# A hybrid decoder layer: the split parts of the key, weight and time-step matrix are kept for all four token tiles

## The chip, the cores and the metric

The kernel runs on one core of one Trainium2 chip. The core has five engines that each work through their own queue in order: TensorE (PE in the rows, its weight loads are PEld), VectorE (DVE), ScalarE (ACT), GpSimd (POOL) and SyncE (SP), which issues the DMA requests of this kernel. The metric is device time of one execution in microseconds (us). Lower is better.

## The reference, cut to what matters

One layer, 2048 tokens of width 1024. One input projection feeds an attention over selected keys and a state-space mixer (SSD); their outputs go through an output projection and an MLP.

```python
u = rms_norm(h, norm_pre_mix)
q, k, v, qi, ki, wi, z, xbc, dt = split(u @ w_in)     # widths 512,128,128,256,64,4,512,1024,8
ki = layer_norm(ki); wi = wi * 4 ** -0.5
attn = sparse_attention(q, k, v, qi, ki, wi, rel_bias)  # each query keeps its 256 best keys by
                                                        # sum_h wi[t,h] relu(qi[t,h] . ki[s])
ssd = ssd_mixer(z, xbc, dt, ...)                        # causal conv, scan over chunks of 128, gate, norm
h = h + rms_norm(concat(attn, ssd) @ w_out)
h = h + rms_norm(square(relu(rms_norm(h) @ w_up)) @ w_down)
```

The change concerns three of the nine outputs of the input projection: the index keys `ki` (64 columns), the index weights `wi` (4) and the time steps `dt` (8). Their 76 columns of `w_in` are one array, `w_misc`, of 1024 x 76.

## The kernel before

All large products are made of fp32 numbers split into a high part and a low rest (fp32r): `split` (lines 228 to 232) writes the high part with ACT (L229) or POOL (L231), by a switch, and the rest with POOL (L232). `mm3` (L257, L260, L261) then multiplies high by high, high weight by low operand, and low weight by high operand into one PSUM bank.

**The stages.** The tokens lie in four tiles of 512. The first stage, some 760 us long, runs `in_proj(t)` for the four tiles one after another. The later stages run the output projection and the MLP tile by tile. `in_proj(t)` makes 21 products with the tile's operand `u`, which has eight slices u[0] to u[7] of 128 rows each; a product `proj` is eight `mm3`, so 24 matmuls. The first product of a tile is the one with `w_misc` (76 rows out, tile `p_mm`, `mi`); then come eight products for `xbc`, two for `qi`, four for `z`, one each for `k` and `v`, and four for `q`. The slices of the next tile are made at the end of a tile by `moving(t + 1)`: for each slice a request `xr<-x_t`, a scaled copy on ACT (L305, L308, L311) and the rest on DVE (L312) or POOL (L309, slices 3, 5 and 7). There are eight buffers `u`, so slice k of the next tile can be written once the last product of the old tile has read slice k. I call the stretch from the last product of one tile to the first product with `w_in` of the next a seam; there are three.

**Weights.** `load_w` (L236 to L248) fetches a matrix in two halves of four slices each: a request `wr<-...` (L246) into one of four raw buffers `wr`, which the eight requests `xr` use too, then `split` into buffers `wh` and `wl`, two of each. `w_misc` goes this way in every tile: in tile 0 with the high part on ACT, in tiles 1 to 3 with both parts on POOL, in all four through the same `wr`, `wh` and `wl` as the other weights.

**Order.** SSD steps (`p_x`, `p_y`, `p_st`, `lm`, `cb`, `si`), the search for the best keys (`p_ix`, `junk_k`, `cnd`) and attention (`p_s`, `p_pt`, `p_o`, `qs`, `tq`) are woven into the products by `weave` with planned times. A scheduler then fixes the order of every engine's queue at build time from priorities and modelled durations; a change at one place so alters the order elsewhere. SP's requests also go out in their fixed order: one that waits for a buffer holds those behind it.

Of the kernel before, what the change touches and what calls it, by code (L numbers as in the profile page):

```python
# [21 lines left out]
P = 128  # L22
# [5 lines left out]
KT = D // P  # L28
# [13 lines left out]
def hybrid_layer(ctx, tc, x, x_t, w_cols, n_post_mix, n_post_mlp, w_in, w_misc, dt_bias, a_log, d_skip,  # L42
# [10 lines left out]
    HI_, HO, HU, HW = "00,11,00,00".split(",")  # L53
    FC, BC = (2,3)
# [4 lines left out]
    WR = 4  # L59
    COMMON = dict(u=8, wr=WR, wl=WL, wh=WL, rsb=1, sc=2, mkk=1, qi=1, ks=2)  # L60
    ATT = dict(c2=2, qs=2)
    FRONT = dict(c4=FC, x24=1, m4=2, m2=3, kc=2, tq=1, mk=1)
    BACK = dict(c4=BC, x8=2, g4=9, m2=2)
    SSD = dict(si=3, cb=2, lm=1, xd=1)
    SIDE = [dict(kc=3, tq=1, mk=1), dict(kc=2, tq=1)]
# [16 lines left out]
    def tl(tag, shape, dt=F32, name=None):  # L82
        pool, bufs, slot = place(tag)
        return pool.tile(shape, dt, tag=name if tag in ("s", "ks", "ssm") else slot, name=name or tag, bufs=bufs)

    def phase(name, sizes, smalls=None, side="left"):
        stack = ExitStack()
        pool = stack.enter_context(tc.tile_pool(name=name, bufs=1, side=side, reuse_waits="tile"))
        use(pool, sizes)
        if smalls:  # L90
            use(pool, {smalls: 2})
        return stack
# [13 lines left out]
    def banks(name, sizes):  # L106
        stack = ExitStack()
        use(stack.enter_context(tc.tile_pool(name=name, bufs=1, space=PSUM, reuse_waits="tile")), sizes)
        return stack
# [11 lines left out]
    scan = phase("scan", SSD, "ssm", "right")  # L121
    front = phase("front", FRONT, "s")
    side_banks = banks("bank0", BANKS[0])
# [103 lines left out]
    def split(dst_hi, dst_lo, src_f, how):  # L227
        if how:
            S.activation(dst_hi, src_f, AF.Copy)  # L229
        else:  # L230
            G.tensor_scalar(dst_hi, src_f, 1.0, 0.0, op0=OP.mult, op1=OP.add)  # L231
        G.tensor_tensor(dst_lo, src_f, dst_hi.bitcast(F32), op=OP.subtract)  # L232

    def load_w(ap, shape, how='00', tag=None):

        n = shape[1] // 2  # L236
        parts = []
        for i in range(2):
            raw = tl("wr", [P, n, shape[2]], name="wr")
            if tag:  # L240
                both = tl(tag, [P, 2, n, shape[2]], F32R, name="w2")
                hi, lo = both[:, 0], both[:, 1]
            else:
                hi = tl("wh", [P, n, shape[2]], F32R, name="wh")
                lo = tl("wl", [P, n, shape[2]], F32R, name="wl")
            SP.dma_start(raw, ap[:, i * n:(i + 1) * n])  # L246
            split(hi, lo, raw, how[i] == '1')
            parts.append((hi, lo))  # L248
        return parts

    state = {"win": "0"}
# [13 lines left out]
    def proj(ap, u, w=None, how='00'):  # L265

        m = ap.shape[-1]
        w = w or load_w(ap, [P, KT, m], how)
        p = pt("mm", "p_mm")
        for k in range(KT):  # L270
            hi, lo = w[k // 4]
            mm3(p[0:m], hi[:, k % 4, :], lo[:, k % 4, :], u[k][:, 0, :], u[k][:, 1, :], k == 0, k == KT - 1)
        return p
# [45 lines left out]

    def in_proj(t):  # L320
        t0 = t * T
        w = None
        if t == 0:
            w = load_w(w_misc, [P, KT, 76], '11')
            moving(0)
        else:
            rsb = row_spread(state["rs", t], TB)
        u = state["u", t]
        scaled = lambda o, p: V.tensor_tensor(o, p, rsb[0:o.shape[0]], op=OP.mult)


        p = proj(w_misc, u, w, how=HI_)
        if t == 0:
            row_scale(0)
            rsb = row_spread(state["rs", 0], "acc")
# [5 lines left out]
        p = pt(TB, "p_tr")  # L341
# [22 lines left out]
        for m in range(8):  # L364
            p = proj(w_in[m], u, how=HI_)
# [9 lines left out]
            if m == 1:  # L375
                p = pt(TB, "p_tr")
# [21 lines left out]
        for m in range(4):  # L398
            p = proj(w_in[8 + m], u, how=HI_)
# [9 lines left out]
        p = proj(w_in[12], u, how=HI_)  # L409
# [8 lines left out]
        p = proj(w_in[13], u, how=HI_)  # L418
# [3 lines left out]
        p = pt(TB, "p_tr")  # L422
# [665 lines left out]
```

## Time and profile before

| what | value |
|---|---|
| median of 3 runs | 2921.4 us (2916.97 to 2927.34) |
| the profiled execution's own time | 2928.29 us |
| its span, first to last instruction | 2926.5 us |
| mean granted TensorE clock | 0.973 of full speed |
| PE busy | 2761.9 us, 94% of the span |
| POOL, DVE, ACT busy | 1762.6, 1642.4, 1481.5 us |
| share of the chain that ended last | PE 67%, DVE 13%, ACT 6%, DMA 5%, issue 4%, POOL 3% |

The profile is of one execution. A row of the timeline gives start, duration, engine, line, operation, output and inputs, shape and count, and in brackets how long the engine had been idle and what ended that. A row of the windows gives the busy time of each engine in one stretch of the span.

### The profile page before, as it was taken

To read this page: it belongs to the slowest core of one execution; us is meant where nothing else is said; L and a number is where in the kernel's file an instruction comes from. 1 tells how busy PE (TensorE), PEld (TensorE's weight loads), DVE (VectorE), ACT (ScalarE), POOL (GpSimd) and SP (SyncE) were. 2 spreads that over 40 slices of the span, in tenths; PEclk is the share of its full clock that TensorE was granted. 3 is DMA by queue.
4 is the path that set the end of the run, shared out by engine and by line. 5 is a ranking of instruction groups with operands and counts; after the bars stand their busy time and mean duration, and the time that the engine had idled before them with its cause. 6 is when DMAs were issued, how large, how long until landed. Compare 5 with 4: busy or idle time off the path is not lost.

```text
span 2926.5 us, 41201 instructions
## 1 busy us (share of the span) xinstructions
PE 2761.9 (94%) x13558; PEld 2250.7 (77%) x13558; DVE 1642.4 (56%) x4106; ACT 1481.5 (51%) x2550; POOL 1762.6 (60%) x1721
## 2 busy tenths in 40 slices
PE   7988989789989999998999999999999999999998
PEld 5766767667768887887787888878888888778886
DVE  5479588888575666747765565666444342511113
ACT  2375477675837575677773847644332332311101
POOL 4666556667666656654456575644564656588775
PEclk8999989999989999999999999999999999999999
DMA  3765654634733333255223222553222225522222
GB/s 128 224 189 151 218 157 149 208 118 160 249 120 119 112 103 102 90 176 180 101 94 98 90 97 79 170 177 102 87 95 81 93 78 177 204 95 97 95 94 86
DMA packets 286741, 383.46 MB, mean 131 GB/s; under 512 B 26520, under 2 KB 151360, under 8 KB 286528
## 3 DMA queue, kind: packets, MB, share of 16 engines
q1 hardware_dynamic: 286528, 380.84, 40.0%
q8 instruction: 107, 1.75, 0.2%
q14 instruction: 106, 0.87, 0.1%
HBM read 316.44 MB, written 64.30 MB: 130 GB/s over the span
## 4 chain that ended last, share of the span: by engine, by line
PE 67%; DVE 13%; ACT 6%; DMA 5%; issue 4%; POOL 3%; SPq 1%; POOLq 0%; DVEq 0%; ACTq 0%
PE p_mm L257 9%; PE p_mm L261 9%; PE p_mm L260 9%; PE p_dn L260 7%; PE p_dn L261 7%; PE p_dn L257 7%; ACT junk_k L610 5%; PE p_o L725 4%; PE p_s L683 4%; PE p_pt L717 3%; POOL wl L232 2%; PE p_ix L591 1%; DVE cnd L618 1%; PE p_acc L260 1%; PE p_acc L257 1%
## 5 line engine op out<-in xcount | busy, mean ns | idle before, releaser
L232 POOL TENSOR_TENSOR wl<-wr,wh 128x512 fp32r<-128x512 f32 (+1 forms) x740 | 987.0, 1335 | 179.6 <-ACT wh L229 107.0
L231 POOL TENSOR_SCALAR wh<-wr 128x512 fp32r<-128x512 f32 x674 | 449.6, 667 | 752.1 <-PE p_mm L260 372.8
L257 PE MATMUL p_mm<-u,wh 128*128 128x512 f32 (+1 forms) x1696 | 685.4, 404 | 47.4 <-ACT u L311 15.4
L261 PE MATMUL p_mm<-u,wl 128*128 128x512 f32 (+1 forms) x1696 | 682.8, 404 | 13.2 <-POOL wl L232 12.9
L260 PE MATMUL p_mm<-u,wh 128*128 128x512 f32 (+1 forms) x1696 | 674.9, 398 | 0.6 <-POOL u L309 0.3
L610 ACT ACTIVATE junk_k<-sc,cnd 128x512 int8<-128x512 f32 (+10 forms) x434 | 576.4, 1328 | 157.8 <-DVE cnd L618 122.2
L257 PEld LDWEIGHTS p_mm<-u,wh 128*128 128x128 f32 (+1 forms) x1696 | 322.9, 190 | 119.3 <-ACT u L311 17.5
L260 PE MATMUL p_dn<-wl,g 128*128 128x512 f32 x1008 | 402.2, 399 | 4.2 <-POOL wl L232 4.2
L261 PE MATMUL p_dn<-wh,g 128*128 128x512 f32 x1008 | 399.5, 397 | 2.7 <-POOL g L836 2.7
L261 PEld LDWEIGHTS p_mm<-u,wl 128*128 128x128 f32 (+1 forms) x1696 | 322.5, 190 | 88.7 <-POOL wl L232 21.3
L260 PEld LDWEIGHTS p_mm<-u,wh 128*128 128x128 f32 (+1 forms) x1696 | 322.6, 190 | 69.6 <-DVE u L312 2.3
L257 PE MATMUL p_dn<-wh,g 128*128 128x512 f32 x1008 | 328.0, 398 | 1.9 <-POOL wh L231 1.3
L834 ACT ACTIVATE r<-r 128x512 f32<-128x512 f32 x128 | 80.4, 629 | 437.1 <-DVE r L833 436.7
L688 DVE CUSTOM_DVE_ANT_0 pp<-p_s,mk 128x512 f32<-128x512 f32 (+3 forms) x320 | 192.5, 607 | 134.3 <-PE p_s L683 130.5
L719 ACT ACTIVATE ppt<-p_pt 128x512 fp32r<-128x512 f32 (+1 forms) x288 | 155.3, 568 | 208.1 <-PE p_pt L717 170.0
L720 DVE TENSOR_TENSOR ppt<-p_pt,ppt 128x512 fp32r<-128x512 f32 (+1 forms) x288 | 182.6, 655 | 129.6 <-ACT ppt L719 126.9
L260 PEld LDWEIGHTS p_dn<-wl,g 128*128 128x128 f32 x1008 | 190.3, 189 | 46.8 <-POOL wl L232 5.5
L261 PEld LDWEIGHTS p_dn<-wh,g 128*128 128x128 f32 x1008 | 190.3, 189 | 43.8 <-POOL g L836 3.1
L257 PEld LDWEIGHTS p_dn<-wh,g 128*128 128x128 f32 x1008 | 185.8, 189 | 42.0 <-POOL wh L231 2.9
L725 PE MATMUL p_o<-ppt,VV 128*128 128x256 f32 x1088 | 211.1, 294 | 1.9 <-DVE ppt L720 1.0
L617 DVE TENSOR_SCALAR keep<-cnt 128x1 int32<-128x1 f32 (+1 forms) x341 | 70.2, 206 | 244.1 <-ACT junk_k L610 242.7
L836 POOL TENSOR_TENSOR g<-r,g 128x512 fp32r<-128x512 f32 x128 | 170.1, 1331 | 53.2 <-ACT g L835 51.9
(253 smaller groups left out, 4177.6 us busy)
## 6 DMA issues: line engine op xcount, KB each, us to landing
wr<-w_up SPq DMA_DIRECT2D x256, 256.0 KB, 2.6
wr<-w_down SPq DMA_DIRECT2D x256, 256.0 KB, 2.6
wr<-w_in SPq DMA_DIRECT2D x160, 256.0 KB, 2.9
tq<-toep_d SPq DMA_DIRECT2D x128, 128.0 KB, 2.6
qs<-q_d SPq DMA_DIRECT2D x256, 64.0 KB, 2.5
wr<-w_out SPq DMA_DIRECT2D x64, 256.0 KB, 3.7
mix<-mix_d SPq DMA_DIRECT2D x32, 512.0 KB, 8.1
q_d<-qp SPq DMA_DIRECT2D x24, 512.0 KB, 3.6
```

Of the source, the lines that this page charges most:

```text
L231: G.tensor_scalar(dst_hi, src_f, 1.0, 0.0, op0=OP.mult, op1=OP.add)
L232: G.tensor_tensor(dst_lo, src_f, dst_hi.bitcast(F32), op=OP.subtract)
L257: m = PE.matmul(o, ah, bh, start=first, stop=False)
L260: PE.matmul(o, ah, bl, start=False, stop=False)
L261: state["mm3"] = PE.matmul(o, al, bh, start=False, stop=last).ins.name
L610: S.activation(junk_k[:, 0:n], scs[j], AF.Sign, bias=bias(j), accum_out=cnt[:, j:j + 1])
L683: PE.matmul(p[:, 0:w], qs[:, var, hh, :], K1[:, g, j0:j0 + w], start=var == 0, stop=var == 1)
L688: V.tensor_tensor_reduce(out=pp[:, j0:j0 + w], in0=p[:, 0:w], in1=mk[:, j0:j0 + w], scale=1.0, scalar=-3e38, op0=OP.add, op1=OP.max, accum ...
L719: S.activation(pg[:, 0, 0:w], p[:, 0:w], AF.Copy)
L720: V.tensor_tensor(pg[:, 1, 0:w], p[:, 0:w], pg[:, 0, 0:w].bitcast(F32), op=OP.subtract)
L725: PE.matmul(po[:, c0:c0 + 256], VV[:, kk, g, :], pg[:, part, j * 256:(j + 1) * 256], start=kk == 0 and part == 0, stop=kk == nb - 1 and pa ...
L836: G.tensor_tensor(gt[:, 1, :], r, gt[:, 0, :].bitcast(F32), op=OP.subtract)
```

## The change

In tile 0 the two halves of `w_misc` are split into buffers of their own (tag `wm`, two buffers of 2 x 4 x 76 fp32, 4.9 KB per partition in all) and all four tiles read them from there. Tiles 1 to 3 make no request for `w_misc` and no split of it. In tile 0 the split itself is the same; only its place is another.

```diff
-    FRONT = dict(c4=FC, x24=1, m4=2, m2=3, kc=2, tq=1, mk=1)
+    FRONT = dict(c4=FC, x24=1, m4=2, m2=3, kc=2, tq=1, mk=1, wm=2)
...
     def in_proj(t):
         t0 = t * T
-        w = None
         if t == 0:
-            w = load_w(w_misc, [P, KT, 76], '11')
+            state["wm"] = load_w(w_misc, [P, KT, 76], '11', "wm")
             moving(0)
...
-        p = proj(w_misc, u, w, how=HI_)
+        p = proj(w_misc, u, state["wm"])
```

One line of source is gone, so lines behind L322 have a number lower by one in the changed kernel. The order of the queues moves at the seams, and in smaller steps elsewhere.

SP's requests at the seam into tile 2, before (`xr` is the last slice of `u`, `qs` and `tq` belong to attention):

```order
L676 DMA tq<-toep_d 128x256
L486 DMA cb<-cs_d_3716 128x512
L570 DMA qs<-q_d 64x2x128 x4
L676 DMA tq<-toep_d 128x256
L393 DMA q_d<-qp 128x2x512
L301 DMA xr<-x_t 128x512
L246 DMA wr<-w_misc 128x304
L676 DMA tq<-toep_d 128x256
L246 DMA wr<-w_misc 128x304
L755 DMA mix_d<-atp 128x4x128
L246 DMA wr<-w_in 128x512
```

and now:

```order
L675 DMA tq<-toep_d 128x256
L485 DMA cb<-cs_d_3702 128x512
L301 DMA xr<-x_t 128x512
L246 DMA wr<-w_in 128x512
L569 DMA qs<-q_d 64x2x128 x4
L675 DMA tq<-toep_d 128x256
L392 DMA q_d<-qp 128x2x512
L246 DMA wr<-w_in 128x512
L675 DMA tq<-toep_d 128x256
L246 DMA wr<-w_in 128x512 x2
```

The last slice and the first half of the first matrix of `w_in` have moved ahead of the four `qs`, one `tq` and the `q_d` request.

POOL at the same seam, before (`u` here is slice 5, then slice 7; the splits of `w_misc` have 304 columns):

```order
L501 TENSOR_TENSOR xd<-xd,ends 128x256
L504 TENSOR_TENSOR cb<-cb,si 128x512
L309 TENSOR_TENSOR u<-xr,u 128x512
L231 TENSOR_SCALAR wh<-wr 128x304
L232 TENSOR_TENSOR wl<-wr,wh 128x304
L231 TENSOR_SCALAR wh<-wr 128x304
L232 TENSOR_TENSOR wl<-wr,wh 128x304
L518 TENSOR_TENSOR st<-st,ends 128x256
L309 TENSOR_TENSOR u<-xr,u 128x512
```

and now:

```order
L231 TENSOR_SCALAR wh<-wr 128x512
L503 TENSOR_TENSOR cb<-cb,si 128x512
L232 TENSOR_TENSOR wl<-wr,wh 128x512
L500 TENSOR_TENSOR xd<-xd,ends 128x256
L309 TENSOR_TENSOR u<-xr,u 128x512
L231 TENSOR_SCALAR wh<-wr 128x512
L232 TENSOR_TENSOR wl<-wr,wh 128x512
L231 TENSOR_SCALAR wh<-wr 128x512
L309 TENSOR_TENSOR u<-xr,u 128x512
L232 TENSOR_TENSOR wl<-wr,wh 128x512
L517 TENSOR_TENSOR st<-st,ends 128x256
```

The four splits of `w_misc` are gone, and splits of the first two matrices of `w_in` stand ahead of slices 5 and 7 in their place.

TensorE at the seam into tile 3, before (with buffer numbers; u_6053 and u_6058 are slices 0 and 1 of tile 3, `p_y` and `p_st` an SSD step):

```order
L514 MATMUL p_y_6096<-lm_5985,xd_6001 64x128
L515 MATMUL p_y_6096<-cb_5984,st_90 64x128
L514 MATMUL p_y_6096<-lm_5985,xd_6001 64x128
L515 MATMUL p_y_6096<-cb_5984,st_90 64x128
L517 MATMUL p_st_6105<-xd_6001 128x256
L257 MATMUL p_mm_6137<-u_6053,wh_6126 76x512
L260 MATMUL p_mm_6137<-u_6053,wh_6126 76x512
L261 MATMUL p_mm_6137<-u_6053,wl_6127 76x512
L257 MATMUL p_mm_6137<-u_6058,wh_6126 76x512
L260 MATMUL p_mm_6137<-u_6058,wh_6126 76x512
```

and now (w2_98 is the kept first half, u_6027 and u_6032 are slices 0 and 1 of tile 3, p_mm_5996 is the last `q` product of tile 2):

```order
L514 MATMUL p_y_5894<-cb_5825,st_90 64x128
L260 MATMUL p_mm_6099<-u_6027,w2_98 76x512
L261 MATMUL p_mm_6099<-u_6027,w2_98 76x512
L261 MATMUL p_mm_5996<-u_4104,wl_5992 128x512
L257 MATMUL p_mm_5996<-u_4109,wh_5991 128x512
L260 MATMUL p_mm_5996<-u_4109,wh_5991 128x512
L261 MATMUL p_mm_5996<-u_4109,wl_5992 128x512
L257 MATMUL p_mm_5996<-u_4115,wh_5991 128x512
L260 MATMUL p_mm_5996<-u_4115,wh_5991 128x512
L261 MATMUL p_mm_5996<-u_4115,wl_5992 128x512
L257 MATMUL p_mm_5996<-u_4120,wh_5991 128x512
L257 MATMUL p_mm_6099<-u_6032,w2_98 76x512
```

The product with `w_misc` has moved from behind two SSD steps to slots inside the last `q` product of the old tile, slice by slice.

## Rows read from the trace of the kernel before

**Rows 1.** The page: busy time by engine, and the last chain by engine.

```profile
PE 2761.9 (94%) x13558; PEld 2250.7 (77%) x13558; DVE 1642.4 (56%) x4106; ACT 1481.5 (51%) x2550; POOL 1762.6 (60%) x1721
PE 67%; DVE 13%; ACT 6%; DMA 5%; issue 4%; POOL 3%; SPq 1%; POOLq 0%; DVEq 0%; ACTq 0%
```

**Rows 2.** Windows: stretch, length, five engines' busy time, granted clock, DMA share, GB/s.

```profile
160.00:190.00 30.00, 20.99 (x111) 15.07 (x110) 20.37 (x66) 25.55 (x70) 19.98 (x21) 0.77 0.67 211
190.00:365.00 175.00, 161.31 (x865) 130.27 (x864) 134.84 (x403) 88.14 (x210) 100.38 (x106) 0.99 0.58 178
365.00:400.00 35.00, 24.31 (x129) 17.77 (x128) 26.55 (x64) 30.04 (x69) 20.33 (x21) 0.76 0.66 207
565.00:600.00 35.00, 25.97 (x134) 19.28 (x134) 24.91 (x56) 30.78 (x62) 25.30 (x28) 0.85 0.56 178
760.00:1200.00 440.00, 420.37 (x2096) 345.06 (x2096) 278.53 (x762) 286.49 (x493) 268.69 (x261) 0.98 0.38 124
```

**Rows 3.** The tile view of w_misc: its requests, and time to landing.

```profile
L246 SPq DMA_DIRECT2D wr<-w_misc x8: 327/403/872, 1.7 to 584.8; - x8
DMA to landing us min/median/max: 2.2/3.0/5.9
```

**Rows 4.** Timeline of SP's requests, seam into tile 2.

```profile
380.33 0.46 SPq L301 DMA_DIRECT2D xr<-x_t  x1
380.84 0.86 SPq L246 DMA_DIRECT2D wr<-w_misc  x1
```

**Rows 5.** Timeline of POOL, seam into tile 2.

```profile
386.82 0.45 POOL L231 TENSOR_SCALAR wh<-wr 128x304 fp32r<-128x304 f32 x1 [2.48 <-DMA wr<-w_misc]
387.35 0.84 POOL L232 TENSOR_TENSOR wl<-wr,wh 128x304 fp32r<-128x304 f32 x1
...
391.53 1.30 POOL L309 TENSOR_TENSOR u<-xr,u 128x512 fp32r<-128x512 f32 x1
```

**Rows 6.** Timeline of PE, seam into tile 2.

```profile
387.32 0.71 PE L257 MATMUL p_mm<-u,wh 128*76 128x512 f32 x1 [3.05 <-POOL wh L231]
...
388.39 0.70 PE L514 MATMUL p_y<-lm,xd 128*64 128x128 f32 x4
...
402.56 0.43 PE L261 MATMUL p_mm<-u,wl 128*76 128x512 f32 x1
```

**Rows 7.** Timeline of DVE, seam into tile 2.

```profile
390.41 0.69 DVE L487 TENSOR_TENSOR lm<-cb,trineg 128x512 f32<-128x512 f32 x1 [4.12 <-PE p_y L515]
```

**Rows 8.** Timeline of the seam into tile 1.

```profile
181.05 1.29 POOL L309 TENSOR_TENSOR u<-xr,u 128x512 fp32r<-128x512 f32 x1
...
184.96 2.30 SPq L246 DMA_DIRECT2D wr<-w_in  x4
...
189.00 0.39 PE L260 MATMUL p_mm<-u,wh 128*76 128x512 f32 x1
...
189.23 0.40 PE L261 MATMUL p_mm<-u,wl 128*76 128x512 f32 x1
```

**Rows 9.** Timeline of the seam into tile 3.

```profile
570.21 0.39 PE L261 MATMUL p_mm<-u,wl 128*128 128x512 f32 x1
...
573.71 1.73 DVE L312 SCALAR_TENSOR_TENSOR u<-xr,cols,u 128x512 fp32r<-128x512 f32 x1 [0.16 <-ACT u L311]
...
586.43 0.99 PE L257 MATMUL p_mm<-u,wh 128*76 128x512 f32 x1
...
590.51 1.28 POOL L309 TENSOR_TENSOR u<-xr,u 128x512 fp32r<-128x512 f32 x1
...
594.31 0.39 PE L261 MATMUL p_mm<-u,wl 128*76 128x512 f32 x1
```

**Rows 10.** Windows of 10 us inside two seams, columns as in rows 2.

```profile
170.00:180.00 10.00, 5.06 (x26) 3.85 (x26) 5.84 (x24) 8.05 (x22) 6.88 (x8) 0.55 0.66 201
375.00:385.00 10.00, 5.05 (x16) 3.04 (x15) 8.19 (x22) 9.24 (x23) 6.92 (x7) 0.54 0.73 233
```

**Rows 11.** Timeline of POOL in tile 0.

```profile
34.93 1.21 POOL L231 TENSOR_SCALAR wh<-wr 128x512 fp32r<-128x512 f32 x2 [6.15 <-issue]
```

## The prediction, made before the changed kernel was run

> **What bounds the kernel now.** I read the page's busy times and its last chain first: PE is busy 94% of the span and carries 67% of the chain [rows 1]. So a gain has to come out of a hole of PE, and the next view is the busy time by stretches, to find the holes. Between the seams PE is busy 161.31 of 175 us at a granted clock of 0.99, and in the stage after the first one 420.37 of 440 us at 0.98 [rows 2]. In the three seams it is busy 20.99 of 30, 24.31 of 35 and 25.97 of 35 us: holes of 9.0, 10.7 and 9.0 us, with the clock at 0.77, 0.76 and 0.85 [rows 2]. The removed work lies exactly there: eight requests for `w_misc`, two in tile 0 and two at each seam [rows 3].
>
> The timelines then show what the seams wait for. Into tile 2: the request for the first half of `w_misc` goes out at 380.84, behind the last slice's request at 380.33 [rows 4]; POOL idles 2.48 us for the landing and splits at 386.82 [rows 5]; PE idles 3.05 us for that split and starts the product at 387.32 [rows 6]. An SSD product stands behind it in PE's queue and runs at 388.39 [rows 6], and DVE idled 4.12 us until that was done [rows 7]. The product's last matmul starts only at 402.56 [rows 6], though slice 7 was complete at 391.53 + 1.30 = 392.83 [rows 5]. Into tile 3 the product runs from 586.43 to 594.31, while the last `q` product of tile 2 started its last matmul at 570.21 [rows 9].
>
> **The change part by part.**
>
> *Removed.* Six requests, and on POOL six pairs of splits at 0.45 + 0.84 = 1.29 us [rows 5], 7.7 us in all. POOL is busy 60% [rows 1]; this is worth something only at the seams, where it stands ahead of slice 7.
>
> *Moved.* The 24 matmuls of the product need only `u` now. Two neighbours start 0.23 us apart (189.00, 189.23 [rows 8]), so a product is 24 x 0.23 = 5.5 us, and the 21 matmuls of slices 0 to 6 are 4.8 us. They can run in the hole while slices are still being made; only slice 7's three are left after it. The first half of the next matrix (`w_in`, 12 matmuls, 2.8 us) also comes a raw buffer and a place in SP's queue earlier. What PE saves at a seam is what goes into the hole, up to the point where the next thing is late.
>
> *Tile 1.* The product ended at 189.23 + 0.40 = 189.6, so the second half of the next matrix could begin at 189.6 + 2.8 = 192.4 at the earliest. Slice 7 is ready at 181.05 + 1.29 = 182.3 [rows 8]. Next late is the second half of the first `w_in`: its request still stands behind eight `qs`, a `tq` and a `cb` in SP's queue, which before had gone by 184.96 [rows 8]. With a landing of 3.0 us [rows 3] and a high split of 0.6 (two in 1.21 [rows 11]) that is 188.6, so 192.4 - 188.6 = 3.8 at best. I take 3, since the low split and attention's matmuls stand there too. Bounds 0 and 4.8.
>
> *Tile 2.* After slice 7 (392.83) PE worked without a wait to 402.56: 9.7 us. Of it about 21 matmuls, 4.8 us, leave for the hole. The SSD product no longer waits behind the missing split, and the last slice's request goes ahead of six others. Against it, splits of `w_in` (0.6 + 1.3 + 0.6) take the place of 2.6 us of `w_misc` splits ahead of slice 7 on POOL: no gain there. The moved `w_in` request can also wait for a raw buffer with four `qs` queued behind it, so attention may get its queries later. I take 5; bounds 0 and 9 (the hole is 10.7).
>
> *Tile 3.* Slice 7 is ready at 590.51 + 1.28 = 591.8 [rows 9]; with three matmuls after it the product ends at 592.5 in place of 594.7, 2.2 us; and the first half of the next matrix, 2.8 us, can be done by then: 5.0. But the new order puts slices 0 and 1 inside the last `q` product. Slice 1 was complete only at 573.71 + 1.73 = 575.4, while that product's last matmul started at 570.21 [rows 9]: up to 5 us on its end, and DVE, ACT and POOL have its output in their queues. I take 4; bounds -5 and 7.
>
> *Tile 0.* The second half of `w_in` was split at 34.93 after POOL had idled 6.15 us [rows 11]; the buffers it needed were held by `w_misc`. They are free now, yet the clock and the row scale also hold PE there. 0.5; bounds 0 and 1.
>
> *After the first stage.* PE is 96% busy in the next stretch [rows 2], so time won before it should reach the end. The whole queue order shifts, and that I cannot price from a row; I allow 6 us either way, about a third of PE's hole of 19.6 us in that stretch.
>
> *Sum.* 3 + 5 + 4 + 0.5 = 12.5 us; the bounds add to -5 and 21.8. The profiled execution took 2928.3 us, 1.8 more than its span, so it would take 2915.8. The median of the runs shown is 6.9 us lower, 2921.4; the gain in microseconds is the same, so **2909**.
>
> **The rivals.**
>
> *ScalarE sets the seams.* ACT is the busiest engine in them: 25.55 of 30, 30.04 of 35 and 30.78 of 35 us [rows 2]. The slices pass through it between the counting steps of the key search. If its queue decides when slice 7 and the SSD steps come, the product moves into the hole but what follows does not move up, and about 2 us remain: 2919. For it: the holes of PE lie where ACT is fullest. Against it: at the seam into tile 2, after slice 7 was there PE had 9.7 us of work without a wait, a third or more of it the product, and that work does leave. The Trainium skill (Perfetto Trace Analysis, "Identifying the Most-Contended Engine") says to optimize the engine with the highest occupancy first; by that rule the change, which relieves POOL and SP, does nothing. The rows agree that ACT is fullest in the seams; whether it decides is what the result will show.
>
> *The clock stays up.* Inside the seams PE is busy about half the time, and the granted clock is 0.55 and 0.54, so mostly at the lower of its two levels, 1.2 GHz [rows 10]. If matmuls spread over the hole keep it at 2.4 GHz, the busy time there shrinks by at most 20.99 x 0.23 + 24.31 x 0.24 + 25.97 x 0.15 = 14.6 us. Half of that on the path gives 7 more: 2902. The Trainium skill (TensorE: Matmul & The Clock Gate, "Why this matters for your kernels") advises to leave no idle gaps between bursts of matmuls, or the clock drops; the trace agrees as to the drop. Against the rival: the slices come one by one, so the hole is broken up, not filled.
>
> *PE stands before a missing slice (slower).* Place: the seams, above all the one into tile 3. PE's queue is in order; a matmul that waits for a slice holds the `q`, SSD and attention matmuls behind it, whose results stand in ACT's and DVE's queues ahead of later slices: a loop that did not exist while the product came last. Price: up to 5 us at a seam (570.2 to 575.4 [rows 9]) and no gain: 2921.4 + 3 x 5 = 2936. It makes the kernel slower by over 0.3% from 3 us lost at each seam. For it: the new order at tile 3. Against it: into tile 1 and tile 2 the order puts most slices where the trace has them complete, and the `q` output is not needed soon.
>
> That the change does not do what it says is out: the six requests and twelve splits are missing from the new order.
>
> **How the numbers follow.** The forecast, 2909, has 0.45, with a range of its own of 2903 to 2914. ScalarE sets the seams, 2919, has 0.30; I put with it that the new order later gives the gain back. The clock, 2902, has 0.10. The slower rival, 2936, has 0.15. A measurement of this kernel can tell about 0.3%, 8.8 us, from no change: faster is below 2912.6, slower above 2930.2. Faster: 0.42 of the forecast's 0.45 and the clock's 0.10, so 0.52. Slower: 0.12 of the slow rival's 0.15. Within: the rest, 0.36. The range that should hold the time 8 times in 10 goes from 2897 (the forecast less 6 and the clock's 7, nearly) to 2930, which leaves out most of the slow rival and a little below.
>
> **What would show each step right or wrong.** Right: the windows of the three seams show PE holes shorter by 3 to 5 us each and the first product with `w_in` of a tile earlier by that much than before, counted from the last `q` product; the product with `w_misc` ends within 1 to 2 us of slice 7; the stretch after 760 us keeps its length. ScalarE's rival: slice 7 comes as late as before and PE's holes move behind the product. The clock's: above 0.9 granted in the seams. The slow rival's: rows of the kept product that idle on `u`, with the last `q` product of tile 2 ending 3 to 5 us later. The forecast is wrong if the first stage ends earlier by less than 6 us, or if the later stages lose what it won.

## The result, and the profile after

The changed kernel takes **2941.4 us** (median of five runs, 2938.8 to 2951.7) where the kernel before takes 2922.5 (median of five, 2917.0 to 2927.3). The ratio is 1.0074 with a 95% interval of 1.0053 to 1.0094: slower by 0.7%, 19 us by the medians. The forecast was 2909, faster by 0.4%; the time lies above its range of 2897 to 2930.

The page of the changed kernel, busy time (compare [rows 1]):

```profile
PE 2766.6 (94%) x13558; PEld 2250.2 (77%) x13558; DVE 1650.0 (56%) x4106; ACT 1479.2 (50%) x2550; POOL 1759.7 (60%) x1709
```

POOL has its twelve instructions less. The span is 2939.6 us in place of 2926.5. Of these 13.1 us PE is busy 4.7 longer for the same matmuls and idle 8.4 longer (2939.6 - 2766.6 = 173.0 against 164.6). The profiled execution of before was one of its longer ones, so the medians lie 19 apart and the traces 13.

To find the place, both spans are cut at the same events: the evacuation by DVE of the last `q` product of a tile, of the second and eighth `xbc` product of a tile, the first evacuation of the output projection, and the evacuation of the last MLP's first product (`r`, the 97th of 128 up products). The last MLP is followed up to a step of its last row scale on DVE. The events of seam 2 and of the end of the stretch behind it, in the timeline of the changed kernel:

```profile
372.72 0.68 DVE L388 SCALAR_TENSOR_TENSOR qf<-p_mm,rsb 128x512 f32<-128x512 f32 x1
...
412.75 0.68 DVE L328 TENSOR_TENSOR raw<-p_mm,rsb 128x512 f32<-128x512 f32 x1
...
488.46 0.68 DVE L328 TENSOR_TENSOR raw<-p_mm,rsb 128x512 f32<-128x512 f32 x1
```

Windows between these events, the kernel before (stretch, length, busy PE, PEld, DVE, ACT, POOL, granted clock, DMA share, GB/s): tile 0, seam 1, seam 2, the stretch behind seam 2, seam 3, the later stages up to the last MLP, and that:

```profile
0.00:165.79 165.79, 140.88 (x568) 105.52 (x570) 88.58 (x193) 64.25 (x117) 91.03 (x98) 0.94 0.56 181
165.79:209.39 43.60, 35.98 (x205) 28.15 (x206) 35.21 (x139) 32.37 (x91) 27.43 (x29) 0.86 0.55 169
372.68:425.17 52.49, 42.35 (x228) 33.06 (x229) 44.55 (x135) 40.60 (x93) 27.48 (x29) 0.84 0.53 164
425.17:479.29 54.12, 51.80 (x265) 41.48 (x264) 51.76 (x138) 40.34 (x88) 31.02 (x34) 0.97 0.37 111
...
575.36:611.13 35.77, 27.97 (x157) 21.39 (x158) 27.49 (x83) 29.34 (x59) 26.26 (x29) 0.88 0.42 134
783.39:2593.42 1810.03, 1751.16 (x8794) 1452.57 (x8792) 1007.63 (x2468) 958.25 (x1490) 1035.17 (x978) 0.98 0.36 117
2593.42:2919.03 325.61, 319.65 (x1368) 257.82 (x1368) 61.39 (x117) 45.94 (x80) 247.85 (x251) 0.99 0.27 91
```

The same seven of the changed kernel:

```profile
0.00:169.23 169.23, 141.28 (x578) 106.45 (x580) 91.00 (x194) 64.30 (x117) 91.08 (x98) 0.98 0.54 177
169.23:211.38 42.15, 33.21 (x179) 24.57 (x173) 33.38 (x130) 30.75 (x86) 24.42 (x24) 0.91 0.51 158
372.72:412.75 40.03, 35.45 (x189) 27.09 (x187) 33.68 (x104) 32.29 (x75) 23.20 (x24) 0.91 0.56 179
412.75:488.46 75.71, 67.24 (x343) 53.31 (x342) 65.89 (x183) 56.10 (x122) 37.28 (x41) 0.91 0.36 109
...
585.47:615.18 29.71, 22.30 (x110) 16.14 (x110) 19.78 (x57) 23.51 (x47) 22.46 (x22) 0.94 0.43 141
789.32:2606.55 1817.23, 1752.69 (x8793) 1450.59 (x8791) 1011.44 (x2468) 954.83 (x1490) 1038.96 (x978) 0.98 0.36 117
2606.55:2932.28 325.73, 318.70 (x1368) 256.65 (x1368) 61.67 (x116) 45.94 (x80) 247.71 (x251) 1.00 0.27 91
```

Read the lengths first: tile 0 +3.4 us, seam 1 -1.5, seam 2 -12.5, the stretch behind it **+21.6**, seam 3 -6.1, the later stages +7.2, the last MLP +0.1; what lies between these stretches adds 0.7. Each kernel has one trace, and between executions of the same order a stretch can differ by a few us (by up to 5 in tile 0, see there), so small differences of one pair are not to be read alone. Then read what filled them. The three seams hold 26, 39 and 47 matmuls fewer than before, while PE's idle time in them (length less busy) goes from 7.6 to 8.9, from 10.1 to 4.6 and from 7.8 to 7.4 us. So most of what the seams lost in length is work that now runs elsewhere, not holes that were filled: of the 112 matmuls, 64 are of one product of the SSD steps, `p_y` (46, 32 and 46 before, 28, 16 and 16 now), and some of the rest are the kept product's own, which now begins inside the last `q` product. Behind seam 2 stand 78 matmuls more, and PE idles 8.5 us in place of 2.3.

### The profile page after: what moved, and what is told of

Read it like the earlier page. It is cut to its first block, busy times and chain, and to the rows that moved or that the text cites. A ratio compares the mean times of both kernels' runs of the same rounds, so it can differ in the third digit from the quotient of the medians.

```text
span 2939.6 us, 41169 instructions
## 1 busy us (share of the span) xinstructions
PE 2766.6 (94%) x13558; PEld 2250.2 (77%) x13558; DVE 1650.0 (56%) x4106; ACT 1479.2 (50%) x2550; POOL 1759.7 (60%) x1709
## 4 chain that ended last, share of the span: by engine, by line
PE 66%; DVE 13%; ACT 7%; DMA 6%; POOL 4%; issue 3%; SPq 1%; POOLq 0%; ACTq 0%; DVEq 0%
PE p_mm L257 9%; PE p_mm L261 9%; PE p_mm L260 9%; PE p_dn L260 7%; PE p_dn L261 7%; PE p_dn L257 7%; ACT junk_k L609 4%; PE p_s L682 4%; PE p_o L724 4%; PE p_pt L716 3%; POOL wl L232 2%; PE p_ix L590 1%; PE p_acc L257 1%; PE p_acc L260 1%; PE p_acc L261 1%
## 5 line engine op out<-in xcount | busy, mean ns | idle before, releaser
L232 POOL TENSOR_TENSOR wl<-wr,wh 128x512 fp32r<-128x512 f32 x732 | 984.2, 1346 | 168.5 <-ACT wh L229 110.9
L257 PE MATMUL p_mm<-u,wh 128*128 128x512 f32 x1664 | 670.6, 403 | 26.6 <-POOL wh L231 7.0
L261 PE MATMUL p_mm<-u,wl 128*128 128x512 f32 x1664 | 669.5, 403 | 10.8 <-POOL wl L232 10.6
L260 PE MATMUL p_mm<-u,wh 128*128 128x512 f32 x1664 | 661.4, 398 | 0.0
L257 PEld LDWEIGHTS p_mm<-u,wh 128*128 128x128 f32 x1664 | 318.7, 192 | 95.6 <-issue 19.1
L261 PEld LDWEIGHTS p_mm<-u,wl 128*128 128x128 f32 x1664 | 318.6, 191 | 86.8 <-POOL wl L232 20.4
L260 PEld LDWEIGHTS p_mm<-u,wh 128*128 128x128 f32 x1664 | 318.7, 192 | 65.3 <-issue 0.2
L697 ACT ACTIVATE pp<-pp,nm 128x128 f32<-128x128 f32 (+15 forms) x128 | 153.4, 1198 | 126.7 <-DVE nm L694 105.8
```

What stands on the lines that cost most here:

```text
L257: m = PE.matmul(o, ah, bh, start=first, stop=False)
L260: PE.matmul(o, ah, bl, start=False, stop=False)
L261: state["mm3"] = PE.matmul(o, al, bh, start=False, stop=last).ins.name
L697: S.activation(pp, pp, AF.Exp, bias=nm, accum_out=den[:, h:h + 1])
```

## The experiments

Three questions were open: whether the order of the queues alone can cost this much, what happens behind seam 2, and what happens in tile 0. All runs of before beside them had medians of 2923.6 to 2925.7 us.

### Is it the order? Two plans, and the product held back

`SS` is the planned time of the SSD steps in `weave`; a shift of 2 us changes no work; it alters the order in which the queues do it.

```diff
-    SS = (90,170)
+    SS = (92,172)
```

> The kernel before with one planner's number changed: the SSD steps are planned 2 us later in every tile (92 to 172 in place of 90 to 170). The same work, no kept parts; only the build-time order moves, by about as many rows as in the changed kernel. Theory A (the changed kernel loses by the order that it happens to get, not by what it does at the seams): this kernel too moves by 8 us or more from the kernel before (2922.5 us), most likely up, 2931 to 2950 us. Theory B (a product that starts slice by slice inside the old tile is itself the loss): the order elsewhere is harmless, so within 5 us of the kernel before, 2917 to 2928. Theory C (DVE at the start of a tile takes the gain back, whatever the order): no seam gain here, so nothing to give back, 2917 to 2928.

Measured: 2947.4 us (2945.4 to 2951.4), 1.0088 of before (1.0071 to 1.0105). A planner's number moved by 2 us costs 23 us against the median beside it (2924.7), more than the change does. Theories B and C, by which the order elsewhere is harmless, miss it.

> The changed kernel with the SSD steps planned 2 us later, as in the run of the kernel before with that edit. Theory A (the order decides): another order, another time; it may come out anywhere from 2912 to 2950 us and moves by 8 us or more from the changed kernel (2941.4) in either direction. Theory B (the early product decides): the early product is still there, so 2936 to 2947. Theory C (DVE takes the gain back): no better than the kernel before, so 2922 to 2947.

Measured: 2922.3 us (2916.6 to 2923.2), 0.999 of before (0.998 to 1.0). With the same edit the changed kernel gains 19 us and lies 25 below its pair. The early product is in it as before, so B falls; C's band, 2922 to 2947, holds it at its very edge.

The next kernel keeps the parts, but its product takes slice 7 first in tiles 1 to 3, so it can't start before the last slice is there:

```diff
-        for k in range(KT):
+        for k in ks:
...
-        p = proj(w_misc, u, w, how=HI_)
+        p = proj(w_misc, u, state["wm"], ks=(7, 0, 1, 2, 3, 4, 5, 6) if t else tuple(range(KT)))
```

> The changed kernel with the product with w_misc taking its slices in the order 7, 0, 1, ... 6 in tiles 1 to 3. Its first matmul then waits for the slice that comes last, so nothing of it can start inside the old tile; the six requests and twelve splits are still gone. Theory B (the early product is the loss): the loss goes, 2915 to 2926 us. Theory A (the order is the loss): the order is another again, so 2915 to 2950, with no tie to where the product stands. Theory C (DVE takes the gain back): the seams lose most of their gain against the changed kernel, raw 16 later by some 5 us, and the end moves by less than that.

Measured: 2966.4 us (2956.2 to 2968.8), 1.0154 (1.0136 to 1.0172), the slowest of all. Holding the product back doesn't bring the time back; it lies even above the band that theory A gave. That is the second run against B, which is close to the forecast's slow rival; since the run also draws a new order, it doesn't show what holding the product back costs in itself.

### More plans, in pairs

The SSD steps 4 us earlier, and the search and attention of the first stage 2 us later, each in both kernels:

```diff
-    SS = (90,170)
+    SS = (86,166)
...
-    PH = 62,100,100,230,172,260,282,430
+    PH = 64,102,102,232,174,262,284,432
```

> The kernel before with the SSD steps planned 4 us earlier in every tile (86 to 166 in place of 90 to 170). Nothing is kept, no work is changed. Theory A (the order that the build happens to find decides, and the plan of the kernel before is a lucky or tuned one): slower than before by 8 us or more, 2931 to 2955 us. Theory B (the kept product itself is the loss): within 5 us of the kernel before, 2918 to 2929; the run with the steps 2 us later, 2947, already speaks against that, and this one shows whether it stands alone.

> The changed kernel with the SSD steps planned 4 us earlier, to be set beside the kernel before with the same edit. Theory A (order alone, keeping worth about nothing): anywhere from 2915 to 2960 us, and above or below its pair with even chances. Theory B (keeping is a loss in itself): above its pair by 10 us or more. Theory D (keeping is worth the forecast's 10 to 12 us, hidden under the order): below its pair by 5 us or more more often than not, as with the steps 2 us later (2922 against 2947).

> The kernel before with the key search and the attention of the first stage planned 2 us later (all eight planned times plus 2); 398 of 10117 rows of PE move, a quarter of what the SSD edits move. Theory A: off the kernel before (2922.5 us) by 5 us or more, rather up, 2928 to 2945. Theory B: 2918 to 2929.

> The changed kernel with the key search and the attention planned 2 us later, to be set beside the kernel before with the same edit. Theory A: anywhere from 2915 to 2960 us, above or below its pair with even chances. Theory B: above its pair by 10 us or more, 2940 to 2950. Theory D: below its pair by 5 us or more, and below the changed kernel's 2941.

Measured: 2954.5 (ratio 1.0073 to 1.0131) and 2954.3 (1.0069 to 1.0131) with the SSD steps earlier; 2950.5 (1.0054 to 1.0117) and 2949.2 (1.0057 to 1.0113) with the search later. The upper end of theory A's 2945 was too low for one of them. In both pairs keeping makes no difference to the whole, so B, which put the kept kernel 10 us or more above its pair, and D, which put it 5 or more below, miss both.

Two further plans of the changed kernel, with the SSD steps 1 and 4 us later (`SS = (91,171)` and `(94,174)`):

> The changed kernel with the SSD steps planned 1 us later in every tile. A further draw of the order. If the time of a kept kernel is a draw from the same band as that of a kernel without (2922 to 2955 so far): 2922 to 2955. If the plan with 2 us later is a region in which keeping pays, close to its 2922.

> The changed kernel with the SSD steps planned 4 us later in every tile. As the run with 1 us later: 2922 to 2955 if the order is a draw, close to 2922 if the plan with 2 us later is a region and not a point.

Measured: 2930.5 us (2925.2 to 2934.8) and 2937.5 (2932.9 to 2940.3). Neither is close to 2922, so the plan with 2 us is a point, not a region.

### Seam 2 and the stretch behind it

The parts kept for tile 2 alone (with `wm=2` in `FRONT`, as in the change):

```diff
+        if t == 1: state['wm'] = load_w(w_misc, [P, KT, 76], HI_, 'wm')
-        p = proj(w_misc, u, w, how=HI_)
+        p = proj(w_misc, u, state['wm'] if t in (1, 2) else w, how=HI_)
```

> The kernel before, but the w_misc parts loaded in tile 1 go into buffers of their own and are kept for tile 2; tiles 0, 1 and 3 fetch and split as before. The order moves in far fewer rows than in the changed kernel (378 of 10117 on PE). So this is the seam into tile 2 alone. The forecast's term for it was 5 us (bounds 0 to 9). Theory A (order elsewhere is the loss): the gain stays, 2912 to 2920 us. Theory B (the early product is the loss): slower than before by a third of the loss seen, 2927 to 2935. Theory C (DVE takes the gain back at the start of tile 2): raw 16 earlier by some 8 us, gone by raw 23, and 2919 to 2926 in all.

Measured: 2937.3 us (2935.5 to 2942.6), 1.0055 (1.0037 to 1.0072). All three misjudged it. Its picture is C's, but stronger: seam 2 takes 40.7 us (52.5 before), and the stretch behind it 77.7 (54.1). What seam 2 wins is more than lost there, as in the changed kernel.

What that stretch holds is seen in the matmuls of one SSD product, `p_y`, in windows of seam 2 and of the stretch behind it (columns PE, PEld and DVE only). Before:

```profile
372.68:425.17 52.49, 3.36 (x32) 2.48 (x32) 1.19 (x4) 0.84 0.53 164
425.17:479.29 54.12, 3.32 (x32) 2.11 (x32) 1.77 (x6) 0.97 0.37 111
```

And in the changed kernel:

```profile
372.72:412.75 40.03, 1.14 (x16) 0.90 (x16) 1.18 (x4) 0.91 0.56 179
412.75:488.46 75.71, 6.06 (x64) 4.45 (x64) 2.38 (x8) 0.91 0.36 109
```

A step has eight of them. Two of four SSD steps have left the seam, and twice as many run behind it as did: two came from the seam and two were drawn forward from later stretches. DVE was busy 51.76 of 54.12 us there before and has 65.89 us of work now, so the stretch could not keep its length. Behind seam 1, too, `p_y` rises, from 32 to 48 matmuls, but DVE's work does not, and the stretch grows by 0.6 us only. All work there, before and then in the changed kernel:

```profile
209.39:266.20 56.81, 51.01 (x285) 41.29 (x284) 52.70 (x160) 36.18 (x98) 31.75 (x35) 1.00 0.52 157
```

```profile
211.38:268.74 57.36, 55.43 (x308) 46.14 (x309) 52.31 (x159) 37.68 (x99) 31.89 (x35) 0.95 0.54 159
```

Over all eighteen kernels the stretch behind seam 2 takes 67 to 79 us in the six with 61 to 64 `p_y` matmuls in it, and 54 to 64 us in the twelve with 16 to 50. One of the six keeps nothing: the kernel before with the search 2 us later, 67.3 us.

Behind seam 2 PE waits for the chains of those steps, of the key search and of the convolution; timeline of PE in the changed kernel:

```profile
435.17 0.47 PE L590 MATMUL p_ix<-KI,qi 128*128 128x512 f32 x1 [2.81 <-DMA qi<-q_d]
436.69 0.79 PE L590 MATMUL p_ix<-KI,qi 128*128 128x512 f32 x1 [1.05 <-DVE sc L595]
...
467.64 0.52 PE L495 MATMUL p_x<-ident,si 128*128 128x128 f32 x3 [1.70 <-DMA si<-s_d]
...
470.09 0.77 PE L257 MATMUL p_mm<-u,wh 128*128 128x512 f32 x1 [1.48 <-DVE pre L373]
```

Over and behind the first two waits the granted clock is 0.80 and 0.69, so part of the time at the lower of its two levels (windows of the changed kernel):

```profile
430.00:440.00 10.00, 6.15 (x26) 4.31 (x25) 10.00 (x29) 9.07 (x20) 4.49 (x5) 0.80 0.48 145
440.00:450.00 10.00, 8.67 (x44) 6.88 (x44) 9.56 (x24) 6.94 (x16) 3.66 (x4) 0.69 0.08 27
```

To tell the displaced steps from the keeping, the SSD steps of tile 1 alone were planned 2 us later, in both kernels:

```diff
-        tasks.append(stask(t, SS[0] + t * TI, SS[1] + t * TI))
+        tasks.append(stask(t, SS[0] + t * TI + 2 * (t == 1), SS[1] + t * TI + 2 * (t == 1)))
```

> The changed kernel with the SSD steps of tile 1 alone planned 2 us later (they run in the second half of tile 1 and the first half of tile 2); the order up to the end of tile 1 stays as it is. Theory F (what the changed kernel won at the seam into tile 2 it lost because its order pushed SSD steps from the seam into the stretch from the second to the last xbc product of tile 2): with those steps planned elsewhere, that stretch takes 58 to 65 us, not 75.7, as in the changed kernel with all SSD steps moved (60.4), and the SSD matmuls in it fall from 112 to below 90. Theory G (keeping itself makes that stretch slow): 73 to 79 us again. The end goes by the order of the rest, 2915 to 2955.

> The kernel before with the SSD steps of tile 1 alone planned 2 us later, as the pair of the changed kernel with that edit. Theory F: the stretch from the second to the last xbc product of tile 2 takes 54 to 65 us here too, and the pair differs there by less than 6 us. Theory G: the pair differs by 12 us or more. Whole time: by all other re-planned kernels, slower than the kernel before, 2930 to 2955.

Measured: 2924.7 us (2920.9 to 2929.0), 0.9994 of before (0.9983 to 1.0004), with kept parts, and 2939.9 (2936.3 to 2942.2), 1.0045, without. Windows of the one with kept parts, seam 2 and the stretch behind it, first all work and then `p_y` alone:

```profile
373.25:415.80 42.55, 37.89 (x212) 29.07 (x212) 37.16 (x110) 34.57 (x81) 25.54 (x26) 0.92 0.56 176
415.80:478.98 63.18, 54.41 (x281) 43.88 (x281) 58.12 (x164) 47.39 (x102) 29.40 (x34) 0.95 0.39 117
...
373.25:415.80 42.55, 2.29 (x32) 1.81 (x32) 1.79 (x6) 0.92 0.56 176
415.80:478.98 63.18, 3.28 (x34) 2.63 (x36) 1.19 (x4) 0.95 0.39 117
```

The `p_y` matmuls are back to 32 and 34, all SSD matmuls behind the seam fall from 112 to 69, and the stretch behind is 63.2 us, in theory F's bounds; G's 73 to 79 falls. But F also wanted the pair to differ by less than 6 there, and it differs by 9.5 (53.7 without kept parts): with the displaced steps 12.5 of the 21.6 us go, not all. Seam 2 is 7.7 shorter in the pair (42.6 against 50.3). Over seam 2 and the stretch behind it together the pair stands at 105.7 against 104.0.

### Tile 0

The parts in buffers of their own in tile 0, and fetched again in tiles 1 to 3; then the opposite, tile 0 as before and kept from tile 1 on (both with `wm=2` in `FRONT`):

```diff
-            w = load_w(w_misc, [P, KT, 76], '11')
+            w = load_w(w_misc, [P, KT, 76], '11', "wm")
```

```diff
+        if t == 1:
+            state["wm"] = load_w(w_misc, [P, KT, 76], HI_, "wm")
+        w = w or state["wm"]
```

> The kernel before, but in tile 0 the parts of w_misc go into buffers of their own (tag wm); tiles 1 to 3 fetch and split as before, so nothing is kept. This is the change's part in tile 0 alone: the buffers wh and wl are free for the second half of the first w_in earlier. Theory E (that freedom costs time in tile 0: POOL splits the second half beside DVE's row scale, and PE takes its twelve matmuls ahead of the transposes of mi, so the softplus chain starts later): tile 0 ends 3 to 5 us later than in the kernel before, as in all four kernels that keep the parts (qf 5 at 169.2 to 173.3 us against 162.5 to 168.1). The forecast's term: 0 to 1 us earlier. The end of the kernel goes by the order of the rest, 2920 to 2955.

> Tile 0 as before; the parts are loaded into their own buffers at the seam into tile 1 and kept for tiles 2 and 3. Theory E: tile 0 ends within 1 us of the kernel before (qf 5 at 165 to 167), where the changed kernel ends it at 169.2. No gain at the seam into tile 1, gains of 1 to 12 us at the seams into tiles 2 and 3 (as in the four pairs so far, mean 4.6 each). The end of the kernel goes by the order of the rest: 2912 to 2950.

Measured: tile 0 ends at 170.8 us with own buffers and nothing kept, and at 165.7 with tile 0 left alone (165.8 before): theory E holds, and the forecast's 0 to 1 us of gain does not. The whole: 2954.2 (1.008 to 1.012) and 2953.8 (1.0074 to 1.0114); the second just over its band.

The other kernels bear it out. In the traces of eight kernels with own buffers in tile 0 the engines have the same order there, and the tile ends at 166.3 to 171.4 us, 169.8 in the mean; in six with the shared buffers, again of one order, at 162.5 to 166.8, 165.3 in the mean. So the loss is 4.5 us, while executions of one order differ by 4 to 5. One of the eight hardly shows it (the changed kernel with the SSD steps 1 us later, 166.3).

Three rows of PE show where it arises: the row scale's spread, the transposes of `mi`, and the wait of a later `xbc` product. With own buffers in tile 0:

```profile
31.09 2.08 PE L290 MATMUL p_rs<-ident,rs 128*128 128x128 f32 x8 [2.70 <-DVE rs L225]
39.37 0.43 PE L343 MATMUL p_tr<-ident,mi 76*128 76x76 f32 x4
50.48 0.76 PE L257 MATMUL p_mm<-u,wh 128*128 128x512 f32 x1 [5.17 <-DVE tails L369]
```

Kept from tile 1 on:

```profile
27.86 2.07 PE L290 MATMUL p_rs<-ident,rs 128*128 128x128 f32 x8 [0.95 <-DVE rs L225]
34.88 0.48 PE L346 MATMUL p_tr<-ident,mi 76*128 76x76 f32 x4
46.36 0.65 PE L257 MATMUL p_mm<-u,wh 128*128 128x512 f32 x1 [2.74 <-DVE rs_y L221]
```

The changed kernel is like the first (DVE, POOL and PE):

```profile
28.68 1.18 DVE L225 SCALAR_TENSOR_TENSOR rs<-rs_u,rs_y 128x4 f32<-128x4 f32 x1
...
28.59 1.26 POOL L232 TENSOR_TENSOR wl<-wr,wh 128x512 fp32r<-128x512 f32 x1
...
29.92 2.07 PE L290 MATMUL p_rs<-ident,rs 128*128 128x128 f32 x8 [2.56 <-DVE rs L225]
...
37.97 0.43 PE L342 MATMUL p_tr<-ident,mi 76*128 76x76 f32 x4
...
49.10 0.77 PE L257 MATMUL p_mm<-u,wh 128*128 128x512 f32 x1 [5.17 <-DVE tails L368]
```

And before, the last step of the row scale was short, the transposes came earlier, and the later wait was half as long:

```profile
28.83 0.16 DVE L225 SCALAR_TENSOR_TENSOR rs<-rs_u,rs_y 128x4 f32<-128x4 f32 x1
...
29.05 2.08 PE L290 MATMUL p_rs<-ident,rs 128*128 128x128 f32 x8 [1.03 <-DVE rs L225]
...
36.25 0.48 PE L343 MATMUL p_tr<-ident,mi 76*128 76x76 f32 x4
...
47.72 0.47 PE L257 MATMUL p_mm<-u,wh 128*128 128x512 f32 x1 [2.74 <-DVE rs_y L221]
```

The buffers that `w_misc` held are free, so POOL splits the second half of the first `w_in` at once, beside DVE's row scale, and PE takes ten of its matmuls between the last with `w_misc` and the transposes of `mi`, where two stood before. The transposes come 1.7 us later, the softplus chain on DVE behind them, and with it the evacuations for which the next products wait. The last step of the row scale is not the mark of it: it took 0.16 us with own buffers and nothing kept, and 1.19 in the kernel kept from tile 1. The mark is how many steps of that chain take over 1.1 us: three in both kernels with own buffers shown here, two in both without, one in the kernel that ended at 166.3. In the means of the fourteen kernels 1.4 of the 4.5 us have arisen when the row scale's spread starts, 1.6 arise between it and the transposes, and 1.6 behind them. Neither the splits beside DVE nor the ten matmuls were taken away alone.

### The best of both

Tile 0 as before, and `w_misc` fetched once more late in tile 0 (at the fourth product of `xbc`) into the kept buffers, so that all three seams are free of it. A second kernel does it at the seventh, with `SS = (92,172)`:

```diff
-        w = None
+        w = state.get('wm')
...
         for m in range(8):
             p = proj(w_in[m], u, how=HI_)
+            if t == 0 and m == 3: state['wm'] = load_w(w_misc, [P, KT, 76], HI_, 'wm')
```

> Tile 0's product with w_misc as before, through the shared buffers; at the fourth product of tile 0 w_misc is fetched and split once more, into the buffers that are kept, and tiles 1 to 3 read them. So all three seams are without requests and splits of w_misc and the start of tile 0 is as before. Theory E: tile 0 ends within 1.5 us of the kernel before (165 to 167.5), and the seams still gain 2 to 12 us each. If the seams' gains held, 2910; by the spread of the kernels so far, 2912 to 2950.

> The kernel that keeps the parts from a second load late in tile 0 (at the seventh product), with the SSD steps planned 2 us later, the plan with which the changed kernel took 2922. Tile 0 without its loss of 5 us (qf 5 at 165 to 167 against 171.3 in the changed kernel with that plan). If the rest keeps its order, 2917; by the spread, 2912 to 2950. It is the candidate to beat both kernels.

Measured: 2948.2 us (2941.8 to 2949.7) and 2953.7 (2948.9 to 2953.9). The second lies above its band of 2912 to 2950. Tile 0 ended at 167.6 and 163.3, about where the kernels with shared buffers end it, so its loss is avoided; the second reached the output projection at 779.0 us, 4.4 ahead of the kernel before, and then took 1839.7 us for the later stages in place of 1810.0. No kernel here beats the one before by more than the measurement can tell.

### What the pairs say together

Five plans, each without and with kept parts, cut at the events above (us, from the traces; the first column is the median):

| plan | median | end of tile 0 | seam 1 | seam 2 | behind seam 2 | seam 3 | output projection begins |
|---|---|---|---|---|---|---|---|
| as it was | 2922.5 / 2941.4 | 165.8 / 169.2 | 43.6 / 42.1 | 52.5 / 40.0 | 54.1 / 75.7 | 35.8 / 29.7 | 783.4 / 789.3 |
| SSD 2 later | 2947.4 / 2922.3 | 166.0 / 171.3 | 42.4 / 39.2 | 47.1 / 42.5 | 60.0 / 60.4 | 40.1 / 35.1 | 788.0 / 781.1 |
| SSD 4 earlier | 2954.5 / 2954.3 | 168.1 / 173.3 | 51.9 / 47.5 | 46.3 / 45.5 | 56.0 / 58.0 | 40.2 / 44.5 | 801.5 / 807.8 |
| search 2 later | 2950.5 / 2949.2 | 162.5 / 171.2 | 43.3 / 43.5 | 46.7 / 46.2 | 67.3 / 78.6 | 42.9 / 31.5 | 802.2 / 798.6 |
| tile 1's SSD 2 later | 2939.9 / 2924.7 | 166.8 / 169.6 | 42.9 / 42.2 | 50.3 / 42.6 | 53.7 / 63.2 | 37.5 / 29.2 | 782.2 / 776.8 |
| mean difference | -4.6 | +5.1 | -1.9 | -5.2 | +9.0 | -5.3 | -0.7 |

The differences of the medians run from -25 to +19 us; the standard error of their mean is 7.5 us, so what keeping is worth over all plans is not settled by five. Without the plan that the kernel before came with, the other four give -25.1, -0.2, -1.3 and -15.2, a mean of -10.5 with a standard error of 6.0: that the forecast's 12 us hold for a plan drawn anew is neither shown nor excluded. What is settled: without kept parts the plan of the kernel before lies 0.45 to 1.02%, 13 to 30 us, below its four neighbours (ratios 1.0045, 1.0085, 1.0088, 1.0102), and an edit that draws a new order gives that up, unless the new one is as good.

The later stages, whose code and planned times no kernel here edits, show the same: from the first evacuation of the output projection to the last MLP the eighteen kernels take 1805 to 1840 us. The last MLP, where no side work is woven in and the main products are held in the order of the code (L258 and L259, `win` 7), takes 325.6 to 328.0 in all. The later stages of two of them, the kernel before and the changed one with the SSD steps 2 us later:

```profile
788.00:2614.10 1826.10, 1754.76 (x8791) 1452.27 (x8791) 1011.06 (x2475) 958.03 (x1496) 1034.55 (x978) 0.98 0.37 116
```

```profile
781.10:2587.93 1806.83, 1747.60 (x8792) 1449.48 (x8791) 1008.83 (x2468) 957.49 (x1490) 1032.44 (x977) 0.98 0.37 118
```

The same matmuls (8791 and 8792 in the rows) take 19.3 us longer in the one, 12 of it PE's idle time (71.3 against 59.2).

## Why the prediction was wrong, point by point

**What bounds the kernel.** Right in that PE is busy 94% and holes of PE are where time can be won. Wrong in what a hole is, see below.

**The forecast's own test.** It was to be wrong if the first stage ended earlier by less than 6 us: the output projection begins 5.9 us later (789.3 against 783.4).

**Tile 0, -0.5 us.** The term failed in sign: +3.4 us, 2.8 to 8.7 in the five pairs, and 4.5 by the fourteen kernels above. The step said that the freed buffers would bring the second half of `w_in` earlier. They did; what that half would then overtake was not asked. POOL's splits fell on DVE's row scale, and ten bulk matmuls stood ahead of the transposes from which the softplus chain starts.

**The seams, -3, -5 and -4 us.** As lengths these were near as means of the pairs, -1.9, -5.2 and -5.3; in this plan they were -1.5, -12.5 and -6.1, the second beyond its bound of 9. The product ran as described; at seam 2 (timeline of the changed kernel) it waits little for slices, and its last matmul starts 2.1 us after slice 7 is complete (390.46 + 1.73 = 392.19):

```profile
375.48 0.46 PE L260 MATMUL p_mm<-u,w 128*76 128x512 f32 x1 [0.23 <-POOL u L309]
...
378.35 0.46 PE L260 MATMUL p_mm<-u,w 128*76 128x512 f32 x1 [0.94 <-DVE u L312]
...
390.46 1.73 POOL L309 TENSOR_TENSOR u<-xr,u 128x512 fp32r<-128x512 f32 x1
...
394.32 0.40 PE L261 MATMUL p_mm<-u,w 128*76 128x512 f32 x1
```

**The step that failed is "what PE saves at a seam is what goes into the hole".** The hole was not free time. SSD, search and attention matmuls used it, in between their waits; the product and the first `w_in` matmuls, which can now go sooner, took the places of SSD steps, and two steps of each seam ran later. PE's idle time in the three seams fell by 4.6 us in all, not by 12. At seam 2 the displaced steps came into the stretch where DVE is busiest, 51.76 of 54.12 us, together with two more from later on; DVE's work there grew by 14.1 us and the stretch by 21.6, with PE waiting 1.05 and 1.48 us for DVE and 2.81 and 1.70 for transfers. The step "where a stall goes, what is late next" was worked out for the next `w_in` request, not for the side work.

**After the first stage, +-6 us.** The term was put on one hole in one stretch. The changed kernel lost 7.2 us there, a little more than that; over all kernels the later stages span 34 us. The uncertainty of a newly drawn order is the largest term of this kernel, and the sum had it as an aside.

**The sum's base.** The forecast took the time of one plan and subtracted. The runs show that this base holds for this plan alone: with four other plans the same kernel takes 2940 to 2955. That could not be read from the profile of one plan, but it could be suspected, since the order moves away from the seams too.

**The rivals.** *ScalarE sets the seams* expected slice 7 as late as before, PE's holes behind the product and about 2 us left. At seam 2 the first two came: slice 7 was complete at 392.2 (392.8 before), and PE idles 8.5 us behind the seam in place of 2.3. It had right, too, that the gain would be given back later. But ACT was not what slice 7 waited for: ACT's copy of it was done at 385.76 + 0.62 = 386.4, and POOL, which had to finish it, stood before a half of `w_in` and split it and part of the next first (ACT and POOL in the changed kernel):

```profile
385.76 0.62 ACT L308 ACTIVATE u<-xr 128x512 fp32r<-128x512 f32 x1
...
387.87 0.62 POOL L231 TENSOR_SCALAR wh<-wr 128x512 fp32r<-128x512 f32 x1 [1.93 <-DMA wr<-w_in]
```

ACT is about as full in seam 2 as before, 32.29 of 40.03 us against 40.60 of 52.49, and the seam is 12.5 us shorter. The Trainium skill (Perfetto Trace Analysis, "Identifying the Most-Contended Engine") says to optimize the fullest engine first. In the 35 us around seam 2 that was ACT [rows 2]; over seam 2 and the stretch behind it DVE was busy 96.3 of 106.6 us, and that is the stretch in which the time was won and lost. *The clock stays up*: it did in the seams, 0.86, 0.84 and 0.88 before against 0.91, 0.91 and 0.94, and fell from 0.97 to 0.91 behind seam 2. *PE stands before a missing slice* gave nearly the time (2936), but not by what happened. The waits on slices are 0.23 and 0.94 us at seam 2, and the last `q` product of tile 1 is evacuated when it was (372.68 and 372.72). At the seam into tile 3, its main place, the waits did come (PE in the changed kernel):

```profile
586.99 0.46 PE L257 MATMUL p_mm<-u,w 128*76 128x512 f32 x1 [1.62 <-ACT u L308]
...
589.70 0.71 PE L260 MATMUL p_mm<-u,w 128*76 128x512 f32 x1 [2.25 <-POOL u L309]
```

They fall behind the last `q` product's evacuation at 585.47, though; counted from the eighth `xbc` product of tile 2 that is 97.0 us in place of 96.1, so 0.9 later and not 3 to 5, and the seam itself is 6.1 us shorter.

**What stays open.** Whether keeping is worth something on average; what in the order makes the later stages 7.2 us longer; and whether DVE alone bounds seam 2 with the stretch behind it, for which DVE would have to be relieved without a new order. That was not tried.

## What to carry to other kernels

Where a build draws the order of the queues, time a change with several plans of both versions before believing either sign: here the order alone is worth 13 to 30 us, beside 19 for the change. Price a hole of PE by its idle time and by which matmuls stand in it, for a product that moves in pushes them out, and ask in which stretch they will land. A buffer that comes free lets bulk work start sooner, and bulk work that starts sooner can overtake the short chain for which everything waits.

## What the runs showed of the hardware

Tiny DVE instructions become long beside POOL. The steps of the row scale have 128x4 elements and take 0.16 us where POOL is idle; the last of them, L225, took 1.18 us in the changed kernel, where POOL's split of 1.26 us ran from 28.59, and 0.16 in the kernel before, where POOL had nothing behind slice 7. L225 ends at 29.86, with POOL's split (29.85). In these rows a POOL instruction so holds one step of a short chain on DVE for up to its own length. The Trainium skill (SBUF — State Buffer, "SBUF: two separate sides") describes a port pair that the two engines lock in turn for a whole instruction, among others for a DVE operation with two inputs in SBUF; the rows agree with that.
